# SBUF placement of a decoder trunk's tiles: weights and activations at multiples of 2048 bytes, the recurrence's tiles at the top, the MLP's tiles below

## The chip, the cores and the metric

The kernel runs on one core of a Trainium2 chip. A core has a matrix engine (PE, with its weight loads listed apart as PEld), a vector engine (DVE), a scalar engine (ACT), a general engine (POOL) and a queue engine (SP) that issues nearly all transfers here. SBUF is the on-chip memory: 128 partitions, each with its own bytes numbered from 0; a tile of 128 x 512 f32 takes 2048 consecutive bytes in every partition. PSUM holds what PE writes. The metric is the device time of one execution in microseconds.

A matmul has two operands in SBUF. The stationary one (128 x 128, 512 bytes per partition) is loaded into PE ahead of the matmul, by an instruction that the profile calls LDWEIGHTS, while the matmul before it is still streaming its moving operand (here 128 x 512, 2048 bytes per partition).

## The reference

One layer of a decoder trunk over 2048 tokens of width 1024, followed by a norm; all in f32:

```python
h = rmsnorm(x, norm_mix_w) * (1 + sc1) + sh1          # sc, sh, g: silu(c) @ ada_w + ada_b
proj = h @ w_in                                       # 1024 -> 3624
o_a = hgrn2_mixer(hq, hf, hi, hg, ...)                # gated linear recurrence, 4 heads, chunks
o_b = dsa_mixer(sq, sk, sv, iq, ik, iw)               # indexer, top-256 keys per query, softmax
o_c = conv_module(cu, ...)                            # GLU, causal depthwise conv, LayerNorm, swish
x = x + g1 * (concat[o_a, o_b, o_c] @ w_out)
h = rmsnorm(x, norm_mlp_w) * (1 + sc2) + sh2
x = x + g2 * (square(relu(h @ mlp_w1)) @ mlp_w2)
return rmsnorm(x, final_norm_w)
```

## The kernel before

Tokens go in four blocks of 512. For each block the normed x is transposed into eight tiles of 128 x 512 and split into a high part `ah` and a low part `al` (both fp32r, 8 buffers each, pool `act`). Each product of f32 matrices is then three fp32r products: high x high, high x low, low x high. Weights are fetched into `wraw`, split by ACT and POOL into `whi` and `wlo`, written to DRAM once (`wk_d`) and read back by later blocks as `wk` into the same buffers (pool `wts`). The program has two stages.

- The in-projection of all four blocks (`in_block`, matmuls of `mm_T`, L424, and `n_part`, L1280). Between its units run the recurrence (`hgrn_gen`), the convolution and, for the first six query blocks, the indexer, top-k and attention with tiles of the pool `tk1`. The recurrence's tiles are in the pool `hgrn`.
- The out-projection and the MLP of the four blocks (`mlp_block`). `mm_T` (L424) makes the hidden layer: stationary a 128 x 128 piece of a weight tile, moving a tile of `ah` or `al`. `wide_part` (L1304) makes the second product and the out-projection: stationary a 128 x 128 piece of a hidden tile (`hh`, `hl`) or of a mixer output (`mh`), moving a weight tile of 128 x 512. In the last block seven of eight groups run as Strassen products (`product`, L1464; stationary a piece of `hc`, moving a weight tile). The remaining query blocks run between these, with tiles of the pool `tk2`.

All addresses in SBUF come from the pools. A pool is opened on the left (upwards from the lowest free byte) or on the right (downwards from the top) and is closed as a stack; tiles lie in it in the order in which the program first asks for them, each on a multiple of 32 bytes. The left side begins with `cst` (constants), then `act`, `wts` and `xio` (tiles of x, `xt` and `tf`). The other pools take turns: `hgrn` (left) and `tk1` (right) live in the first stage; `mlp` (right) takes the place of `tk1` when the last of its query blocks is done, `mlpacc` (the accumulator `acc`) and `tk2` (both left) take the place of `hgrn`. A pool that takes over memory waits for the last users of what lay there, tile by tile.

Where the tiles that feed the large matmuls start, in bytes of a partition (buffers of one kind follow each other at multiples of 2048):

| tile | pool | role at L424 | role at L1304 and L1464 | start | start modulo 2048 | start modulo 128 |
|---|---|---|---|---|---|---|
| ah, al | act | moving | - | 20448 | 2016 | 96 |
| wraw, whi, wlo, wk | wts | stationary | moving | 53216 | 2016 | 96 |
| hh, hl, mh, hc | mlp | - | stationary | 185216 | 896 | 0 |

At L424 the moving tile and every stationary piece (512 bytes apart) are a whole multiple of 128 bytes away from each other. At L1304 and L1464 the stationary piece starts 32 bytes past a whole multiple of 128 from the moving tile. The accumulator `acc` starts at 98528; `qi`, `ki`, `qs`, `kc`, `vc` and `pT` of the attention start at other remainders in `tk1` than in `tk2`.

The order of the instructions is set by a scheduler that plays a timeline of the program when it is built; the row lists of the engines below come from there.

`exact_rows` (its three words `cd`, `rj`, `c4`) is a branch for queries whose search does not close; it is taken only when a register says so.

Of the kernel before, what the change touches and what calls it, by code (L numbers as in the profile page):

```python
# [8 lines left out]
F32 = mybir.dt.float32  # L9
# [5 lines left out]
U32 = mybir.dt.uint32  # L15
# [5 lines left out]
P = 128  # L21
# [57 lines left out]
def trunk(ctx, tc, x, c, ada_w, ada_b, norm_mix_w, norm_mlp_w, w_in, hg_lb_logits,  # L79
# [12 lines left out]
    cst = ctx.enter_context(tc.tile_pool(name="cst", bufs=1))  # L92
# [48 lines left out]
    def dram(shape, dt, name):  # L141
# [23 lines left out]
                    fill=NEG_BIG, base=0, channel_multiplier=1)  # L165
# [262 lines left out]
    def in_norm(b):  # L428
        xts = []
        for t in range(4):  # L430
            xt = xp.tile([P, D], F32, tag="xt", bufs=4, name=nm("xt"))
            dma(xt, x2d[b * TB + t * P:b * TB + (t + 1) * P, :])
            dump = xp.tile([P, D], BF16, tag="tf", bufs=2, name=nm("xdump"))
            rs = rstd_of(xt, D, dump, "x")
            V.tensor_scalar(xt, xt, rs, None, op0=OP.mult)
            xts.append(xt)
        return xts


    S1 = ExitStack()  # L440
    S1b = ExitStack()
    hp = S1.enter_context(tc.tile_pool(name="hgrn", bufs=1))
    tp = S1b.enter_context(tc.tile_pool(name="tk1", bufs=1, side="right"))

    iw_s = cst.tile([P, 16, 8], F32, name="iw_s")
    S_st = [hp.tile([P, P], F32, name=f"S_st{h}") for h in range(HH)]
# [14 lines left out]
    zq = cst.tile([P, 14], F32, name="zq")  # L461
    gq_ = cst.tile([P, 14], F32, name="gq_")
    i8 = cst.tile([P, 8], F32, name="i8")

    def search_consts():


        w = hp.tile([P, 5, 14], F32, tag="cu", bufs=2, name="sconst")
        ii = hp.tile([P, 14], mybir.dt.int32, tag="fb", bufs=FBB, name="sint")
        na, p_, q_, a_, b_ = [w[:, i] for i in range(5)]  # L470
        G.iota(ii, pattern=[[P, 14]], base=2 * P + 1, channel_multiplier=1)
        V.tensor_copy(na, ii)
        V.reciprocal(p_, na)
        V.tensor_scalar(gq_, p_, 0.683, None, op0=OP.mult)
        V.tensor_scalar(p_, p_, float(TOPK), None, op0=OP.mult)
        V.tensor_scalar(q_, p_, -1.0, 1.0, op0=OP.mult, op1=OP.add)
        V.memset(na, LAM)
        G.tensor_tensor(a_, p_, na, OP.pow)
        G.tensor_tensor(b_, q_, na, OP.pow)
        V.tensor_tensor(zq, b_, a_, OP.subtract)  # L480
        V.tensor_scalar(zq, zq, 5.0633, None, op0=OP.mult)
        V.reciprocal(p_, p_)
        V.reciprocal(q_, q_)
        V.tensor_tensor(a_, a_, p_, OP.mult)
        V.tensor_tensor(b_, b_, q_, OP.mult)
        V.tensor_tensor(a_, a_, b_, OP.add)
        V.tensor_tensor(gq_, gq_, a_, OP.mult)
        i8i = hp.tile([P, 8], mybir.dt.int32, tag="fb", bufs=FBB, name="i8i")
        G.iota(i8i, pattern=[[1, 8]], base=0, channel_multiplier=0)
        V.tensor_scalar(i8, i8i, 0.5, None, op0=OP.add)  # L490
# [265 lines left out]
    def ada_gen():  # L756
        for sec, dst in ((2, None), (4, a2), (3, sh2), (5, None)):
            for c0 in range(0, D, AW):
                acc = hp.tile([P, AW], F32, tag="ada", bufs=1, name=nm("adacc"))
                yield from ada_part(hp, "adw", AB, acc, sec, c0, AW)  # L760
                if dst is None:
                    pt = ps_xp(13)
                    T.matmul(pt[:1, :AW], ones, acc, start=True, stop=True)
                    row = hp.tile([1, AW], F32, tag="adw", bufs=AB, name=nm("adrow"))
                    dma(row, ada_b[0:1, sec * D + c0:sec * D + c0 + AW])
                    V.tensor_tensor(row, pt[0:1, :AW], row, OP.add)
                    dma(g_d[sec][:, c0:c0 + AW], row)
                else:
                    ada_col(acc, sec, c0, AW, dst)
            if sec == 4:  # L770
                ada_scale(a2, "nmlp")
# [9 lines left out]
    def nkeys(j):  # L781
        return (j + 1) * P
# [43 lines left out]
    def exact_rows(k, j, s, bt, dump, cum, cnt, d):  # L826


        n = nkeys(j)
        bv = bt[:, :n]  # L830
        cd, rj, c4 = [k.t([P, 1], U32, tag, 1) for tag in ("cd", "rj", "c4")]
        V.tensor_copy(bv.bitcast(U16), s.bitcast(U16).rearrange("p (n two) -> p n two", two=2)[:, :, 1])
        V.memset(cd, 0xBFFFFFFF)
        V.memset(c4, 0x40000000)
        V.tensor_scalar(dump, s, 0.0, 0.0, op0=OP.is_ge, op1=OP.add, accum_out=cnt)
        V.tensor_scalar(rj, cnt, float(TOPK), None, op0=OP.is_ge)
        V.copy_predicated(cd, rj, c4)
        for bit in range(30, 15, -1):
            V.tensor_scalar(dump, bv, cd.bitcast(BF16)[:, 1:2], 0.0, op0=OP.is_ge, op1=OP.add, accum_out=cnt)
            V.tensor_scalar(rj, cnt, float(TOPK), float(1 << bit), op0=OP.is_lt, op1=OP.mult)  # L840
            V.tensor_scalar(cd, cd, 1 << (bit - 1), rj, op0=OP.bitwise_xor, op1=OP.bitwise_xor)
        cdh = cd.bitcast(U16)
        sm = k.t([P, 6], F32, "sm", 1)
        hv, neg, sgn, off, need, zc = [sm[:, i:i + 1] for i in range(6)]
        V.tensor_copy(hv, cdh[:, 1:2])
        V.tensor_scalar(neg, hv, 32768.0, None, op0=OP.is_ge)
        V.tensor_scalar(sgn, neg, -2.0, 1.0, op0=OP.mult, op1=OP.add)
        V.tensor_scalar(off, neg, 65535.0, None, op0=OP.mult)
        V.tensor_scalar(dump, bv, cd.bitcast(BF16)[:, 1:2], 0.0, op0=OP.is_gt, op1=OP.add, accum_out=cnt)
        V.tensor_scalar(need, cnt, -1.0, float(TOPK), op0=OP.mult, op1=OP.add)  # L850
        z = cum.bitcast(U16)[:, :n]
        V.tensor_scalar(z, s.bitcast(U16).rearrange("p (n two) -> p n two", two=2)[:, :, 0], sgn, off,
                        op0=OP.mult, op1=OP.add)
        V.scalar_tensor_tensor(z, bv.bitcast(U16), hv, z, op0=OP.is_equal, op1=OP.mult)
        V.memset(zc, 32768.0)
        for bit in range(15, -1, -1):
            V.tensor_scalar(bv, z, zc, 0.0, op0=OP.is_ge, op1=OP.add, accum_out=cnt)
            V.tensor_scalar(cnt, cnt, need, float(1 << bit), op0=OP.is_lt, op1=OP.mult)
            V.tensor_scalar(zc, zc, float(1 << (bit - 1)) if bit else 0.0, cnt,
                            op0=OP.add, op1=OP.subtract)  # L860
        V.tensor_scalar(zc, zc, sgn, off, op0=OP.mult, op1=OP.add)
        V.tensor_copy(cdh[:, 0:1], zc)
        v = cd.bitcast(F32)
        V.tensor_scalar(dump, s, v, 0.0, op0=OP.is_gt, op1=OP.add, accum_out=cnt)
        V.tensor_scalar(cnt, cnt, -1.0, float(TOPK), op0=OP.mult, op1=OP.add)
        V.tensor_scalar(bv, s, v, None, op0=OP.is_equal)
        V.tensor_tensor_scan(cum[:, :n], bv, bv, 0.0, op0=OP.add, op1=OP.max)
        V.scalar_tensor_tensor(bv, cum[:, :n], cnt, bv, op0=OP.is_le, op1=OP.mult)
        V.scalar_tensor_tensor(dump, s, v, bv, op0=OP.is_gt, op1=OP.add)
        V.memset(d, TOPK - AIM - (PASSES - 1) * STEP)  # L870
# [316 lines left out]
    S2 = ExitStack()  # L1187
    k1 = TK(tp, J1 * P, SB)

    def add_topk(k, js):  # L1190
        for j in js:
            queues["idx"].append(index_gen(k, j))
            queues["tk"].append(topk_gen(k, j))
# [402 lines left out]
    for b in range(NB):  # L1596
        def nxt(b=b):
            if b + 1 < NB:
                xq.append(in_norm(b + 1))
        for ev in in_block(b, xq[b], nxt):  # L1600
            if ev == "idx":
                if b == 0:
                    add_topk(k1, (2, 3))
                if b == 1:
                    add_topk(k1, range(4, J1))
                    queues["ada"].append(ada_gen())
            elif ev == "qkv":
                pass
            elif ev == "prep":
                drain("ada")  # L1610
                drain_bg()
                S1b.close()
                mp = S2.enter_context(tc.tile_pool(name="mlp", bufs=1, side="right", reuse_waits="tile"))
                prep_out(0)
            else:
                step()
            if ev == "qkv":
                qdone.append(b)
                if b == 0:
                    queues["at"] += [attn_gen(k1, 0), attn_gen(k1, 1)]  # L1620
# [4 lines left out]
    SP.close()  # L1625
    px["p"] = S2.enter_context(tc.tile_pool(name="psy", bufs=1, space=PSUM, reuse_waits="tile"))
    px["ax"] = AXB
    mq = S2.enter_context(tc.tile_pool(name="mlpacc", bufs=1, reuse_waits="tile"))
    S3 = ExitStack()
    tp2 = S3.enter_context(tc.tile_pool(name="tk2", bufs=1, reuse_waits="tile"))  # L1630
    k2 = TK(tp2, 2048, SB)
    add_topk(k2, ORDER)
    rates.update({"idx": R2[0], "tk": R2[1], "at": R2[2]})
# [33 lines left out]
```

## Time and profile before

| | |
|---|---|
| median of 3 runs | 2909.93 us (2903.92 to 2911.09) |
| the profiled execution, its own time | 2909.95 us |
| its span, first to last instruction | 2908.2 us |
| mean granted clock of PE | 0.984 |
| DMA packets, bytes | 428074, 688.61 MB, 237 GB/s over the span |
| matmul records of 128 x 512 at L424, L1304, L1464 | 5280, 3072, 588 |

The profiled execution lies 0.02 us from the median, so a sum made against its span carries over: 1.7 us lie outside the span. Durations of matmuls in the profile overlap, since their ends are modelled; how far apart they start is read from the timeline and from stretches in which one kind runs alone.

### The profile page before, as it was taken

The numbers are of one execution on the slowest core, as the hardware profiler recorded it, in microseconds if no ns is written. First come the engines' busy times: TensorE is split into PE (matmuls) and PEld (weight loads), VectorE is DVE, ScalarE is ACT, GpSimd is POOL, SyncE is SP. The second block draws the span as 40 slices with busy tenths as digits, with TensorE's granted clock in tenths as the row PEclk, the third lists the DMA queues.
The fourth block names the chain that finished last, engine by engine and source line by source line (L and its number), as shares of the span: only waits on it lengthen the run. The fifth ranks groups of instructions, "written<-read, shape, count | busy, mean of one in ns | idle before, by whom it ended". The sixth has DMA issues, their size and how long they took to land.

```text
span 2908.2 us, 42801 instructions
## 1 busy us (share of the span) xinstructions
PE 2781.8 (96%) x14116; PEld 2306.0 (79%) x14116; DVE 1676.6 (58%) x3514; ACT 1239.7 (43%) x2630; POOL 1086.4 (37%) x1051
## 2 busy tenths in 40 slices
PE   5999998999999989999999999999999998999997
PEld 4888887888788777888777888887788887777776
DVE  6695697777465437656757637477662221254455
ACT  4436444533311244555556444354643332343323
POOL 7444111212100445666665222234422223345444
PEclk9999999999999989999999999999999999999999
DMA  9987676667655668898888776677867666686676
GB/s 292 291 268 243 215 234 190 218 209 245 202 183 180 221 218 255 272 291 284 292 266 295 231 221 216 202 243 258 289 211 237 200 226 197 217 284 209 224 235 206
DMA packets 428074, 688.61 MB, mean 237 GB/s; under 512 B 43383, under 2 KB 171452, under 8 KB 427836
## 3 DMA queue, kind: packets, MB, share of 16 engines
q1 hardware_dynamic: 427680, 685.67, 72.9%
q8 instruction: 113, 1.85, 0.3%
q14 instruction: 125, 1.02, 0.1%
q10 hardware_dynamic: 156, 0.07, 0.0%
HBM read 532.74 MB, written 152.84 MB: 236 GB/s over the span
## 4 chain that ended last, share of the span: by engine, by line
PE 41%; DMA 5%; DVE 4%; POOL 1%; issue 1%; ACT 0%; SPq 0%; POOLq 0%; DVEq 0%; ACTq 0%
PE mm L1304 10%; PE mm L424 9%; PE ax L424 7%; PE ax L1304 6%; PE mm L1464 4%; PE at L965 1%; PE po L999 1%; DMA wk<-wk_d 1%; PE at L987 1%; PE ix L808 1%; DMA tr<-in_mlp_w_dram 1%; PE at L1304 1%; DVE s L815 1%; DVE cum L917 1%; POOL wk L376 1%
## 5 line engine op out<-in xcount | busy, mean ns | idle before, releaser
L424 PE MATMUL mm<-ah,wk 128*128 128x512 f32 x1920 | 513.2, 399 | 4.1 <-DVE slo L537 1.7
L424 PEld LDWEIGHTS mm<-ah,wk 128*128 128x128 f32 x1920 | 355.7, 190 | 78.5 <-DVE slo L537 2.0
L318 POOL TENSOR_TENSOR wlo<-wraw,whi 128x512 fp32r<-128x512 f32 x210 | 285.8, 1380 | 245.2 <-ACT whi L317 133.6
L997 POOL TENSOR_TENSOR pT<-L,pT 128x512 fp32r<-128x512 f32 (+3 forms) x160 | 193.3, 1210 | 374.9 <-ACT pT L996 194.3
L815 DVE SCALAR_TENSOR_TENSOR s<-r,iw_s,s 128x512 f32<-128x512 f32 (+3 forms) x266 | 239.2, 899 | 104.2 <-ACT r L810 95.6
L424 PE MATMUL mm<-al,wk 128*128 128x512 f32 x960 | 262.4, 395 | 0.0
L967 DVE CUSTOM_DVE_ANT_0 L<-at,bias 128x512 f32<-128x512 f32 (+3 forms) x152 | 93.6, 619 | 206.0 <-PE at L965 156.7
L424 PEld LDWEIGHTS mm<-al,wk 128*128 128x128 f32 x960 | 178.3, 189 | 36.0
L1304 PE MATMUL mm<-wk,hh 128*128 128x512 f32 x640 | 197.8, 398 | 1.5 <-ACT tf L286 1.1
L810 ACT ACTIVATE r<-ix 128x512 f32<-128x512 f32 (+3 forms) x256 | 133.2, 554 | 151.6 <-PE ix L808 113.0
L317 ACT CAST whi<-wraw 128x512 fp32r<-128x512 f32 x210 | 122.1, 620 | 162.6 <-DMA wraw<-in_mlp_w_dram 47.9
L273 POOL TENSOR_TENSOR hl<-hr,hh 128x512 fp32r<-128x512 f32 x96 | 129.6, 1351 | 161.3 <-ACT hh L265 159.5
L424 PE MATMUL ax<-ah,wk 128*128 128x512 f32 x720 | 187.1, 393 | 1.4 <-DMA wk<-wk_d 1.4
L588 DVE SCALAR_TENSOR_TENSOR cx<-hc,cvc,cx 128x512 f32<-128x512 f32 x232 | 173.7, 749 | 2.0
L917 DVE TENSOR_SCALAR_CACHE_REDUCE cum<-s,ssm 128x384 bf16<-128x384 f32 (+13 forms) x112 | 165.3, 1476 | 7.3 <-POOL s L819 5.2
L995 ACT COPY L<-at 128x512 f32<-128x512 f32 (+3 forms) x160 | 82.8, 522 | 180.6 <-PE at L987 179.0
L424 PEld LDWEIGHTS ax<-ah,wk 128*128 128x128 f32 x720 | 134.2, 188 | 31.2 <-ACT hc L1438 1.8
L1464 PE MATMUL mm<-wk,hc 128*128 128x512 f32 x588 | 148.4, 397 | 4.9 <-DVE acc L1472 4.9
L981 ACT ACTIVATE L<-L,nmx 128x512 f32<-128x512 f32 (+3 forms) x160 | 103.8, 650 | 97.9 <-DVE nmx L976 97.7
L1304 PEld LDWEIGHTS mm<-wk,hh 128*128 128x128 f32 x640 | 117.9, 188 | 27.4 <-ACT tf L286 1.6
L1464 PEld LDWEIGHTS mm<-wk,hc 128*128 128x128 f32 x588 | 109.4, 188 | 35.3 <-DVE acc L1472 8.7
L1304 PE MATMUL ax<-wk,hh 128*128 128x512 f32 x384 | 123.8, 400 | 1.7 <-DMA wk<-wk_d 1.4
(364 smaller groups left out, 6096.4 us busy)
## 6 DMA issues: line engine op xcount, KB each, us to landing
wk<-wk_d SPq DMA_DIRECT2D x776, 256.0 KB
wk<-wk_d SPq DMA_DIRECT2D x196, 512.0 KB
wk_d<-whi SPq DMA_DIRECT2D x210, 256.0 KB
wk_d<-wlo SPq DMA_DIRECT2D x210, 256.0 KB
wraw<-in_mlp_w_dram SPq DMA_DIRECT2D x68, 512.0 KB
kc<-sk_d SPq DMA_DIRECT2D x112, 256.0 KB
vc<-v_d SPq DMA_DIRECT2D x112, 256.0 KB
adw<-in_ada_w_dram SPq DMA_DIRECT2D x128, 128.0 KB
```

Source lines behind the costliest of these rows:

```text
L273: e.tensor_tensor(lo[:, i:j], src[:, i:j], hi[:, i:j].bitcast(F32), OP.subtract)
L317: A.copy(hi, src)
L318: G.tensor_tensor(lo, src, hi.bitcast(F32), OP.subtract)
L424: T.matmul(ps, ww[k], aa[k], start=(n == 0 and k0 == 0), stop=(n == len(order) - 1 and k1 == NK))
L588: V.scalar_tensor_tensor(acc if w < TAPS - 1 else total, hc[:, w:w + TB], cvc[:, m, w:w + 1], acc, op0=OP.mult, op1=OP.add)
L810: A.activation(r[:, :w], ps[:, :w], AF.Relu, scale=32.0 ** -0.5)
L815: V.scalar_tensor_tensor(s[:, c0:c0 + w], r[:, :w], iw, s[:, c0:c0 + w], op0=OP.mult, op1=OP.add)
L917: V.tensor_scalar(dump, s, t, -AIM - i * STEP, op0=OP.is_ge, op1=OP.add, accum_out=d)
L981: A.activation(lt[:, :w], lt[:, :w], AF.Exp, bias=nmx, accum_out=sm[:, cb:cb + 1])
L997: G.tensor_tensor(pT[:, :nt, 1], lv, pT[:, :nt, 0].bitcast(F32), OP.subtract)
L1304: T.matmul(ps, aa[f][:, tok * P:(tok + 1) * P], ww[i], start=(first and n == 0), stop=(last and n == 5))
L1464: T.matmul(bank[t], aa[:, k, t * P:(t + 1) * P], ww[k], start=(i in (0, 2, 4) and n == 0), stop=(n == 5), skip_group_check=True)
```

## The change

The sides of the pools are exchanged: `hgrn` opens on the right and `tk1` on the left; later `mlp` on the left, in the place of `tk1`, and `mlpacc` and `tk2` on the right, in the place of `hgrn`. A tile of 32 bytes (`fill`) is added to the constants, so that everything behind them moves up by 32 bytes. The three words of `exact_rows` become columns of one tile.

```diff
-    hp = S1.enter_context(tc.tile_pool(name="hgrn", bufs=1))
-    tp = S1b.enter_context(tc.tile_pool(name="tk1", bufs=1, side="right"))
+    hp = S1.enter_context(tc.tile_pool(name="hgrn", bufs=1, side="right"))
+    tp = S1b.enter_context(tc.tile_pool(name="tk1", bufs=1))
...
     i8 = cst.tile([P, 8], F32, name="i8")
+    cst.tile([P, 8], F32, name="fill")
...
-        cd, rj, c4 = [k.t([P, 1], U32, tag, 1) for tag in ("cd", "rj", "c4")]
+        words = k.t([P, 3], U32, "words", 1)
+        cd, rj, c4 = [words[:, i:i + 1] for i in range(3)]
...
-                mp = S2.enter_context(tc.tile_pool(name="mlp", bufs=1, side="right", reuse_waits="tile"))
+                mp = S2.enter_context(tc.tile_pool(name="mlp", bufs=1, reuse_waits="tile"))
...
-    mq = S2.enter_context(tc.tile_pool(name="mlpacc", bufs=1, reuse_waits="tile"))
+    mq = S2.enter_context(tc.tile_pool(name="mlpacc", bufs=1, side="right", reuse_waits="tile"))
     S3 = ExitStack()
-    tp2 = S3.enter_context(tc.tile_pool(name="tk2", bufs=1, reuse_waits="tile"))
+    tp2 = S3.enter_context(tc.tile_pool(name="tk2", bufs=1, side="right", reuse_waits="tile"))
```

The starts after the change:

| tile | start before | start after | after, modulo 2048 | after, modulo 128 |
|---|---|---|---|---|
| ah, al | 20448 | 20480 | 0 | 0 |
| wraw, whi, wlo, wk | 53216 | 53248 | 0 | 0 |
| tf, xt, tr, xo | 77792 | 77824 | 0 | 0 |
| hh, hl, mh, hc | 185216 | 98560 | 256 | 0 |
| acc | 98528 | 212960 | 2016 | 96 |

So at L424 the moving tile and the stationary piece keep their distance, a whole multiple of 128. At L1304 and L1464 the distance becomes a whole multiple of 128 too (before: 32 past one).

Apart from the three words, which become one tile, no engine's sequence changes: the same instructions stand in the same order. What changes besides the addresses is which semaphores a few instructions wait for where one pool takes over the memory of another. The largest such place is on SP at the begin of the MLP of the first block, where `tk2` takes the memory of `hgrn`. `qi`, `ki`, `qs`, `kc` and `vc` are tiles of the first query block in `tk2`, `mx_d` is the last output of the recurrence; names in brackets are semaphores (DMAHW: transfers, PE_49: the matrix engine). Before:

```order
L107 DMA mx_d_3_122<-r_11503 128x512 [waits DMAHW1_49,DVE_49]
L107 DMA qi_11653<-iq_d_76 32x8x128 [waits DMAHW2_49,PE_49]
L107 DMA qi_11653<-iq_d_76 32x8x128 [waits DMAHW3_49]
L107 DMA qi_11653<-iq_d_76 32x8x128 [waits DMAHW4_49]
L107 DMA ki_11658<-ki_d_87 96x512 [waits DMAHW5_49]
L107 DMA qs_12996<-sq_d_80 64x4x128 [waits DMAHW6_49]
```

And now:

```order
L107 DMA mx_d_3_122<-r_11496 128x512 [waits DMAHW1_49,DVE_49]
L107 DMA qi_11646<-iq_d_76 32x8x128 [waits DMAHW2_49]
L107 DMA qi_11646<-iq_d_76 32x8x128 [waits DMAHW3_49]
L107 DMA qi_11646<-iq_d_76 32x8x128 [waits DMAHW4_49]
L107 DMA ki_11651<-ki_d_87 96x512 [waits DMAHW5_49,PE_49]
L107 DMA qs_12987<-sq_d_80 64x4x128 [waits DMAHW6_49]
```

The wait for PE has moved from the first `qi` to `ki`; in the same way it moves a little further on from the first `vc` to the first `kc`. On DVE the first write of `s` (L814 now, L813 before) gains a wait for two transfers and loses none; on ACT, POOL and DVE some twenty other instructions at such places wait for fewer or for other transfers.

## The prediction

> **What bounds the kernel now.** I read the busy shares first, then the slices.
>
> ```profile
> PE 2781.8 (96%) x14116; PEld 2306.0 (79%) x14116; DVE 1676.6 (58%) x3514; ACT 1239.7 (43%) x2630; POOL 1086.4 (37%) x1051
> PE   5999998999999989999999999999999998999997
> ```
>
> PE is busy for 96% of the span, in nearly every slice for nine tenths or more; no other engine passes 58%. All PE idle time together is 2908.2 - 2781.8 = 126 us. So what a change of addresses does to PE's own pace counts almost in full, and what it does to the other engines counts only where PE then waits. The second view is the sum of one line's matmuls over the whole span.
>
> ```profile
> 0.00:2910.00 2910.00, 781.47 (x3072) 0.98 0.73 237
> 0.00:2910.00 2910.00, 148.35 (x588) 0.98 0.73 237
> 0.00:2910.00 2910.00, 1301.69 (x5280) 0.98 0.73 237
> ```
>
> These are L1304, L1464 and L424 in this order: 3072 + 588 + 5280 = 8940 matmuls of 128 x 512, the bulk of PE's time. Their durations in the view by line (min/median/max in ns) differ:
>
> ```profile
> L424 PE MATMUL mm<-ah,wk x1920: 387/389/796, 261.3 to 2568.5; 128*128 128x512 f32 x192
> L424 PE MATMUL mm<-al,wk x960: 387/389/628, 261.6 to 2566.7; 128*128 128x512 f32 x192
> ...
> L1304 PE MATMUL mm<-wk,hh x640: 388/394/505, 1597.7 to 2543.3; 128*128 128x512 f32 x160
> ...
> L1304 PE MATMUL mm<-wk,mh x288: 388/394/482, 1432.7 to 2494.4; 128*128 128x512 f32 x144
> ...
> L1464 PE MATMUL mm<-wk,hc x588: 388/394/505, 2574.2 to 2869.3; 128*128 128x512 f32 x196
> ```
>
> The same size and type takes 389 ns at L424 and 394 ns at L1304 and L1464, whatever the tile. Ends are modelled, so I check it by starts. In the timeline of PE two stretches meet where each kind runs alone and no idle time stands between:
>
> ```profile
> 2475.32 3.19 PE L1304 MATMUL mm<-wk,mh 128*128 128x512 f32 x13
> ...
> 2494.68 2.00 PE L424 MATMUL mm<-ah,wk 128*128 128x512 f32 x8
> ...
> 2516.46 0.60 PE L281 MATMUL mm<-ident,x 128*128 128x128 f32 x4
> ...
> 2475.32:2494.67 19.35, 19.35 (x84) 1.00 0.66 220
> 2494.68:2516.45 21.77, 21.77 (x96) 1.00 0.86 293
> ...
> 2839.83 0.40 PE L424 MATMUL ax<-ah,wk 128*128 128x512 f32 x1
> 2840.07 2.96 PE L1464 MATMUL mm<-wk,hc 128*128 128x512 f32 x12
> 2842.87 0.63 PE L424 MATMUL ax<-ah,wk 128*128 128x512 f32 x2
> ```
>
> L1304: 83 starts (the count of 84 holds the one still running when the stretch begins) from 2475.32 to 2494.68, **233.3 ns** each. L424: 96 from 2494.68 to 2516.46, **226.9 ns**. L1464: 12 in 2842.87 - 2840.07 = 2.80 us, 233.3 ns. The granted clock is 1.00 in both stretches, and the transfers are heavier (293 against 220 GB/s) in the faster one, so neither the clock nor the transfers make the 6.4 ns. What differs is the kind of work and the addresses: at L424 moving tile and stationary piece are a whole multiple of 128 bytes apart, at L1304 and L1464 they are not (the table of starts).
>
> **The change part by part.** *The exchange of sides and the 32 bytes of fill.* No instruction is added or moved, so each term is a pace. At L1304 and L1464 the distance between the moving tile and the stationary piece becomes a whole multiple of 128, as at L424. My reading is that the weight load of the next matmul, which runs while a tile streams, costs the stream some cycles at the old distance and few at a multiple of 128. Then these 3072 + 588 = 3660 matmuls take L424's pace: 3660 x 5 ns (medians) = **18.3 us**; by the dense stretches 3660 x 6.4 = 23.4 us. I take the medians, since most of these matmuls stand among others and not in dense runs. L424 keeps its distance and so its pace: 0.
>
> How much reaches the end? PE's waits and the densest stage tell:
>
> ```profile
> PE at L1304 <- DMA wk<-wk_d: 7.4, 3, 5.6
> PE mm L1304 <- DVE acc L1557: 4.9, 3, 4.0
> PE mm L1464 <- DVE acc L1472: 4.9, 8, 1.4
> ...
> 1200.00:1550.00 350.00, 177.43 (x698) 129.44 (x697) 0.99 0.88 279
> 1550.00:1900.00 350.00, 159.85 (x622) 113.84 (x620) 1.00 0.73 234
> 1900.00:2250.00 350.00, 170.68 (x672) 122.86 (x672) 1.00 0.75 247
> ```
>
> The largest waits at L1304 are 7.4 us for weights and 4.9 for the accumulator, of 781 us. If PE gets 2% quicker there, the weight transfers are late next. From 1550 us on they are busy for 0.73 to 0.75 of the time and have room. From 1200 to 1550 us the share is 0.88; there I count nothing as gained: 698 x 5 ns = 3.5 us. That leaves 18.3 - 3.5 = **14.8 us**. Were the cover gone everywhere, half might be lost.
>
> *The same addresses for the other engines.* ACT and POOL already run one operation at different remainders:
>
> ```profile
> L317 ACT CAST whi<-wraw 128x512 fp32r<-128x512 f32 x210 | 122.1, 620 | 162.6 <-DMA wraw<-in_mlp_w_dram 47.9 <-PE mm L424 32.5 <-DMA wraw<-in_w_in_dram 19.2
> L265 ACT CAST hh<-hr 128x512 fp32r<-128x512 f32 x96 | 59.6, 624 | 2.2
> L318 POOL TENSOR_TENSOR wlo<-wraw,whi 128x512 fp32r<-128x512 f32 x210 | 285.8, 1380 | 245.2 <-ACT whi L317 133.6 <-PE mm L424 38.5 <-PE mm L1280 21.6
> L273 POOL TENSOR_TENSOR hl<-hr,hh 128x512 fp32r<-128x512 f32 x96 | 129.6, 1351 | 161.3 <-ACT hh L265 159.5 <-DMA wk<-wk_d 1.7
> ```
>
> At 2016 modulo 2048 (first and third row) and at 896 (the others) they take 620 and 624 ns, 1380 and 1351 ns: 2% at most. At remainder 0 the trace has no row; by these I put it between -2% and +2% of engines that are 43% and 37% busy, under PE: 0 us.
>
> *The waits where pools take over.* On SP `ki` now waits for PE where `qi` did.
>
> ```profile
> L748 PE MATMUL ax<-ident,hu x64: 270/272/477, 174.4 to 1078.4; 128*128 128x128 f32 x64
> L622 DVE SCALAR_TENSOR_TENSOR cu<-cacc,cols,cu x8: 742/752/753, 301.4 to 1033.0; 128x512 f32<-128x512 f32 x8
> ...
> 1080.12 1.41 SPq L107 DMA_DIRECT2D qi<-iq_d  x3
> 1081.57 0.45 SPq L107 DMA_DIRECT2D ki<-ki_d  x1
> ```
>
> The recurrence's last matmul starts at 1078.4 us and takes 0.3; `ki` is issued at 1081.57, so the wait is over before it is reached. Queued behind it on SP are `qs` and the stores of `wk_d`, which the same holds for. The first write of `s` now waits for transfers of tiles such as the convolution's `cu`, last made at 1033.0 us, also long landed. I take 0; bounds: -1.4 us (the longest wait of SP there, one issue of `qi`, gone) to +1.4 (the same, gained).
>
> *The three words.* The lines of `exact_rows` have no row in the trace: the branch isn't taken. 0.
>
> *Attention in new places.* Distances of `qi`, `qs`, `vc` to the tiles before them change in both directions. It is some hundred weight loads behind a tile of 512; at 6.4 ns a hundred are 0.6 us, either way: 0.
>
> **Sum:** 2909.95 - 14.8 = 2895.1, said as **2895 us**; the execution is 0.02 us from the median, so nothing is added. Own range of this case: -23.4 (dense pace, all of it kept) to -9 (half of 18.3 lost): 2886.5 to 2901.
>
> **The rivals.** *No effect.* The 6.4 ns may belong to the kind of work: L424 adds 24 matmuls into one PSUM tile in a row, L1304 and L1464 six at a time, with activations as the stationary operand and weights as the moving one. One set of rows speaks for it:
>
> ```profile
> L1280 PE MATMUL mm<-whi,ah x96: 277/283/668, 81.4 to 221.9; 128*128 128x256 f32 x96
> ...
> L1280 PE MATMUL mm<-whi,hh x80: 278/282/286, 2870.1 to 2890.0; 128*128 128x256 f32 x80
> ```
>
> At L1280, with 256 columns, the stationary piece of `hh` (off by 32) is no slower than that of `ah` (a multiple of 128): 282 against 283 ns. Against it: each kind loads one stationary piece per matmul, so PE's steps are the same; and the single L424 matmul ahead of the L1464 run, whose stream meets the load of a piece of `hc`, takes 2840.07 - 2839.83 = 0.24 us, some ten ns above L424's own pace, though its own work is L424's. The timeline rounds to 0.01 us, so this is a hint and no proof. Time: 2909.95, between 2906 and 2914 with what runs vary. The Trainium skill's page "SBUF — State Buffer", section "Who interferes with whom", speaks for this rival: it gives PE two independent read ports, one for the moving operand and one for weight loads, and says that PE never waits on anyone. By it the sum would be 0; the trace shows two paces for one size, but no row says whether the addresses make them.
>
> *Slower: the weight tile's own address counts, not the distance.* At L1304 and L1464 every stationary piece starts on a multiple of 128 bytes and is slow; at L424 it starts 96 past one and is fast. The rows fit this as well. After the change L424's pieces start on multiples of 128 too: 5280 x 5 ns = 26.4 us are added, nothing is gained at L1304: 2936. It decides as soon as a round start alone is enough. Against it: at L1280 pieces of `hh` start on multiples of 128 and cost nothing (282 ns). I hold the distance for likelier, since two reads that meet need two addresses.
>
> *Faster still: the start of the moving tile counts.* 512 columns take 226.9 ns; 256 take 120.0 (below), so 256 columns are 106.9 and each matmul has 226.9 - 213.8 = 13.1 ns that its columns don't need.
>
> ```profile
> 2882.92 0.64 PE L1280 MATMUL ax<-wlo,hh 128*128 128x256 f32 x4
> 2883.40 1.12 PE L1280 MATMUL ax<-whi,hh 128*128 128x256 f32 x8
> 2884.36 0.64 PE L1280 MATMUL ax<-wlo,hh 128*128 128x256 f32 x4
> ```
>
> (12 matmuls in 2884.36 - 2882.92 = 1.44 us.) All moving tiles of weights and activations start 32 bytes before a multiple of 2048 now and on one afterwards. If that took a quarter of the 13.1 ns, 8940 x 3.3 = 29 us would come on top: 2866; all of it would be 117 us. For it: no row has a tile at 0. Against: nothing shows that these nanoseconds are reading.
>
> **How the numbers follow.** Forecast (2886.5 to 2901) 0.54; no effect, within 2906 to 2914, 0.21; slower by the weight's own address 0.15; faster still 0.10. A measurement of this kernel can tell about 0.3%, 8.7 us, from no change. The forecast and the last case lie beyond it: faster 0.64; no effect: same 0.21; slower 0.15. The range takes the forecast, the case of no effect with its variation, and the case of faster still down to its quarter: 2866 to 2916. It leaves out the slower case and more than half of the faster one, together 2 in 10.
>
> **What would show it.** Right: medians at L1304 and L1464 fall from 394 to about 389, dense stretches from 233.3 to about 227 ns, L424 stays at 389 and 226.9. No effect: all medians stay. Slower: L424 rises to 394. Faster still: L424 falls below 387. If the medians fall and the time does not, the waits of PE for `wk` or `acc` at L1304 have grown by what was gained. The forecast is wrong at its root if L1304 keeps 394 ns.

## The result and the profile after

| | before | after |
|---|---|---|
| median | 2910.51 us (2903.92 to 2912.61, 4 runs) | 2892.19 us (2887.88 to 2895.25, 4 runs) |
| ratio, 95% interval | | 0.9946 [0.9927, 0.9964] |
| span of the profiled execution | 2908.2 us | 2886.1 us |

By the medians the kernel is 18.3 us faster, by the ratio 15.7 us; the forecast was 2895 us, 15 us faster. Timed again later beside other kernels, it was 11.2 us faster by the medians, 2896.68 against 2907.87 us, and 14.0 us by the ratio, 0.9952 [0.9935, 0.997]. Lines behind the diff have moved: L1304 is L1306 now, L1464 is L1466; L424 keeps its number.

The busy shares and the slices of PE, after:

```profile
PE 2757.0 (96%) x14116; PEld 2297.4 (80%) x14116; DVE 1671.6 (58%) x3514; ACT 1240.7 (43%) x2630; POOL 1086.6 (38%) x1051
PE   5999998999999989999999999999999999999997
```

PE's busy time fell from 2781.8 to 2757.0 us, 24.8 us, with the same 14116 instructions. The other engines stand where they stood to within 5 us. PE's idle time is 2886.1 - 2757.0 = 129 us, against 126 before: 3 us more. The durations by line (min/median/max in ns; first and last start in us):

```profile
L424 PE MATMUL mm<-ah,wk x1920: 387/389/632, 259.3 to 2548.4; 128*128 128x512 f32 x192
...
L1306 PE MATMUL mm<-wk,hh x640: 387/389/499, 1586.1 to 2523.3; 128*128 128x512 f32 x160
...
L1306 PE MATMUL mm<-wk,mh x288: 387/389/485, 1421.9 to 2475.3; 128*128 128x512 f32 x144
...
L1466 PE MATMUL mm<-wk,hc x588: 387/389/504, 2554.1 to 2846.7; 128*128 128x512 f32 x196
```

394 ns has become 389 at L1306 and L1466; L424 keeps 389. The busy time of L1306, L1466 and L424 over the whole span, in this order:

```profile
0.00:2920.00 2920.00, 771.47 (x3072) 0.99 0.73 236
0.00:2920.00 2920.00, 144.99 (x588) 0.99 0.73 236
0.00:2920.00 2920.00, 1295.07 (x5280) 0.99 0.73 236
```

Against the rows of before these are -10.0, -3.4 and -6.6 us. The same dense stretch as in the prediction, in the timeline of PE (start, length, line, operation):

```profile
2456.70 3.15 PE L1306 MATMUL mm<-wk,mh 128*128 128x512 f32 x13
...
2475.56 1.98 PE L424 MATMUL mm<-ah,wk 128*128 128x512 f32 x8
...
2497.32 0.60 PE L281 MATMUL mm<-ident,x 128*128 128x128 f32 x4
```

And by windows, the first with L1306 alone, the second with L424 alone (length, busy time of PE and count, the same of PEld, granted clock, DMA share, GB/s):

```profile
2456.70:2475.56 18.86, 18.86 (x84) 15.39 (x82) 1.00 0.67 222
...
2475.56:2497.34 21.78, 21.78 (x96) 17.84 (x95) 1.00 0.84 294
```

83 starts at L1306 in 18.86 us are **227.2 ns** each (233.3 before); 96 at L424 in 2497.32 - 2475.56 = 21.76 us are 226.7 (226.9 before). The two kinds of work now run at one pace, at the same granted clock of 1.00 and under the same load of transfers as before.

The waits of PE that the prediction named show that no new wait took the gain:

```profile
PE at L1306 <- DMA wk<-wk_d: 7.3, 4, 4.5
PE mm L1466 <- DVE acc L1474: 6.1, 7, 1.9
...
PE mm L1306 <- DVE acc L1559: 5.1, 3, 4.0
```

They were 7.4, 4.9 and 4.9 us.

**Where in the span the time came from.** Four starts divide the program: the last matmul of the recurrence (`ax<-ident,hu`), the first and the last `mm<-wk,hh`, and the last `mm<-wk,hc`. For the changed kernel the first of them is here (the others stand above):

```profile
L749 PE MATMUL ax<-ident,hu x64: 270/272/474, 174.3 to 1068.9; 128*128 128x128 f32 x64
```

The last `hu` starts at 1068.9 us, 9.5 us earlier than before. Of the matmuls with a new pace only the 192 for the first part of the out-projection have run by then; at 4.5 ns each they explain 0.9 us. Most of the 9.5 us is there even before the first of them starts (first row before, second after):

```profile
L1304 PE MATMUL at<-whi,mh x64: 389/394/499, 962.0 to 1014.8; 128*128 128x512 f32 x64
L1306 PE MATMUL at<-whi,mh x64: 387/389/499, 954.6 to 1006.6; 128*128 128x512 f32 x64
```

In a second profiled execution of the same kernel (c1_after below) this lead is missing:

```profile
L749 PE MATMUL ax<-ident,hu x64: 270/273/476, 174.3 to 1077.7; 128*128 128x128 f32 x64
L1306 PE MATMUL mm<-wk,hh x640: 387/389/526, 1597.0 to 2537.2; 128*128 128x512 f32 x160
L1466 PE MATMUL mm<-wk,hc x588: 387/389/713, 2568.0 to 2860.3; 128*128 128x512 f32 x196
```

So most of the early 9.5 us are not the change's. The mean granted clock was 0.987 in the first of these two executions and 0.984 in the second, as in the profile of before:

```profile
core 0: 2886.1 us, clock 0.987
```

```profile
core 0: 2898.5 us, clock 0.984
```

In the 31 runs of the kernel before that stand beside the first four experiments, time and granted clock go together (correlation -0.82, 2.1 us less for each 0.001 of clock), so 0.003 are some 6 us. One profile of each kernel would have credited them to the change. By these rows, as means over executions with the old and the new pace at L1306:

| stage | before, b0, e8 | after, c1, e2, c2 | gain |
|---|---|---|---|
| start to the last `hu` | 1079.4 us | 1075.1 us | 4.3 |
| to the first `mm<-wk,hh` | 518.9 | 518.1 | 0.8 |
| to the last `mm<-wk,hh` | 947.6 | 940.1 | 7.6 |
| to the last `mm<-wk,hc` | 326.0 | 323.0 | 3.0 |

Within one column the values spread by 6 to 10 us in the first stage, so its 4.3 us are no finding; by 1 to 2 us in the second, 3 to 6 in the third and 1 in the fourth. The second stage is the one under heavy transfers (share 0.88 between 1200 and 1550 us, before and after); it holds 966 matmuls of L1304 and gave nearly nothing. The split by stages is weak, though. The kernel e3 below is back at the slow pace and shows 1079.6, 519.1, 942.6 and 324.3 us; e1 and e9, also slow, show 515.1 and 515.4 us in the second stage, less than any execution at the new pace. So stages move by 3 us and more for reasons that these rows don't show, and what follows rests on the paces and on whole times.

### The profile page after: what moved, and what is told of

It reads as the page before. It is cut to its first block, busy times and chain, and to the rows that moved or that the text cites. A ratio compares the mean times of both kernels' runs of the same rounds, so it can differ in the third digit from the quotient of the medians.

```text
span 2886.1 us, 42799 instructions
## 1 busy us (share of the span) xinstructions
PE 2757.0 (96%) x14116; PEld 2297.4 (80%) x14116; DVE 1671.6 (58%) x3514; ACT 1240.7 (43%) x2630; POOL 1086.6 (38%) x1051
## 4 chain that ended last, share of the span: by engine, by line
PE 45%; DMA 4%; DVE 4%; POOL 2%; issue 1%; ACT 1%; SPq 0%; POOLq 0%; DVEq 0%; ACTq 0%
PE mm L1306 11%; PE mm L424 10%; PE ax L424 7%; PE ax L1306 6%; PE mm L1466 3%; PE at L967 2%; PE po L1001 2%; PE at L989 1%; PE ix L809 1%; DMA wk<-wk_d 1%; DMA tr<-in_mlp_w_dram 1%; PE at L1306 1%; DVE s L816 1%; POOL wk L376 1%; DVE cum L919 1%
## 5 line engine op out<-in xcount | busy, mean ns | idle before, releaser
L424 PE MATMUL mm<-ah,wk 128*128 128x512 f32 x1920 | 509.4, 396 | 4.9 <-ACT tf L286 1.9
L424 PEld LDWEIGHTS mm<-ah,wk 128*128 128x128 f32 x1920 | 353.6, 188 | 77.7 <-ACT tf L286 2.1
L424 PE MATMUL mm<-al,wk 128*128 128x512 f32 x960 | 262.3, 395 | 0.0
L424 PEld LDWEIGHTS mm<-al,wk 128*128 128x128 f32 x960 | 177.9, 188 | 35.4
L1306 PE MATMUL mm<-wk,hh 128*128 128x512 f32 x640 | 196.0, 395 | 2.1 <-ACT tf L286 1.1
L424 PE MATMUL ax<-ah,wk 128*128 128x512 f32 x720 | 185.4, 391 | 1.8 <-ACT hc L1440 1.4
L424 PEld LDWEIGHTS ax<-ah,wk 128*128 128x128 f32 x720 | 134.1, 188 | 30.2 <-ACT hc L1440 1.8
L1466 PE MATMUL mm<-wk,hc 128*128 128x512 f32 x588 | 145.0, 392 | 6.9 <-DVE acc L1474 6.1
L1306 PEld LDWEIGHTS mm<-wk,hh 128*128 128x128 f32 x640 | 118.0, 188 | 26.8 <-ACT tf L286 1.7
L1466 PEld LDWEIGHTS mm<-wk,hc 128*128 128x128 f32 x588 | 109.4, 188 | 34.1 <-DVE acc L1474 10.0
L1306 PE MATMUL ax<-wk,hh 128*128 128x512 f32 x384 | 122.6, 397 | 1.5 <-DMA wk<-wk_d 1.1
```

The lines of the kernel that those rows point to most:

```text
L424: T.matmul(ps, ww[k], aa[k], start=(n == 0 and k0 == 0), stop=(n == len(order) - 1 and k1 == NK))
L1306: T.matmul(ps, aa[f][:, tok * P:(tok + 1) * P], ww[i], start=(first and n == 0), stop=(last and n == 5))
L1466: T.matmul(bank[t], aa[:, k, t * P:(t + 1) * P], ww[k], start=(i in (0, 2, 4) and n == 0), stop=(n == 5), skip_group_check=True)
```

## The experiments

Theories. **Distance**: the pace of a 128 x 512 matmul depends on how far the stationary piece lies from the moving tile, modulo 128 as the prediction says, or another period. **Round start**: a start on a multiple of 2048 makes it. **Place**: the MLP's tiles low and the rest high. Distances below are the start of the stationary piece less that of the moving tile, modulo 256; before it is 0 at L424 and 160 at L1304 and L1464, after it is 0 at all.

**e1_fill_only**: the sides of before, with the fill and the words; the distance at L1306 is 128.

```diff
     i8 = cst.tile([P, 8], F32, name="i8")
+    cst.tile([P, 8], F32, name="fill")
...
+        words = k.t([P, 3], U32, "words", 1)
+        cd, rj, c4 = [words[:, i:i + 1] for i in range(3)]
```

> The pools stay on the sides of before; only the 32 bytes of fill and the three words in one tile are taken from the change. Low tiles then start at 0 modulo 2048, the MLP's tiles stay at 185216, and the distance from moving tile to stationary piece at L1304 and L1464 is 0 modulo 128 (128 modulo 256). Distance theory (the pace follows the distance modulo 128): median 389 ns at both lines, 2888 to 2897 us, the whole gain. Round-start theory (the low tiles' start at a multiple of 2048 is what counts): the same 389 and 2892. Place theory (the MLP's tiles must lie low, the others high): 394 ns as before, 2910. A distance theory with a period of 256 would also give about 394.

Measured 2901.09 us, ratio 0.9974 [0.9953, 0.9995]. Medians by line:

```profile
L1306 PE MATMUL mm<-wk,hh x640: 387/394/505, 1594.2 to 2542.2; 128*128 128x512 f32 x160
```

The slow pace stays at a distance of 128: the period is 256, not 128, and low tiles at 2048 alone don't bring the fast pace. That the time fell by some 8 us all the same (0.0026 of 2910) is taken up under e9.

**e2_no_fill**: the changed kernel without the fill; low tiles at 2016 modulo 2048, all distances 0.

```diff
-    cst.tile([P, 8], F32, name="fill")
```

> The change without its 32 bytes of fill: low tiles at 2016 modulo 2048 as before, the MLP's tiles just above them at 98528, so that the distance at L1304 and L1464 stays 0 modulo 128 though no tile starts on a round number. Distance theory: median 389 ns, 2888 to 2897 us, the whole gain. Round-start theory: 394 ns, about 2910. Place theory: 389, about 2892.

Measured 2897.5 us, ratio 0.9964 [0.995, 0.9979]; busy 771.71 us at L1305 (L1306 of the changed kernel), 145.03 at L1465, with medians of 389 ns. Round start falls.

**e3_mlp_32**: the changed kernel with 32 bytes ahead of the MLP's tiles; place and round starts as after, the distance at L1306 and L1466 is 32.

```diff
                 mp = S2.enter_context(tc.tile_pool(name="mlp", bufs=1, reuse_waits="tile"))
+                mp.tile([P, 8], F32, name="shift")
```

> The change with 32 bytes more ahead of the MLP's tiles (98592): low tiles still at 0 modulo 2048, the distance at L1306 and L1466 becomes 32 modulo 128 as it was before. Distance theory: median back at 394 ns at both lines, 3660 x 5 to 6.4 ns = 18 to 23 us lost, 2907 to 2915 us; L424 stays at 389. Round-start theory and place theory: 389 ns, about 2892.

Measured 2906.06 us, ratio 0.9997 [0.9978, 1.0015]: no gain over before is left, and the time lies just below the 2907 to 2915 us expected.

```profile
L1306 PE MATMUL mm<-wk,hh x640: 389/395/503, 1598.7 to 2541.3; 128*128 128x512 f32 x160
...
L1466 PE MATMUL mm<-wk,hc x588: 389/395/504, 2572.1 to 2865.6; 128*128 128x512 f32 x196
```

32 bytes take the pace back at just these two lines (L424 keeps 389 ns). Place falls too.

**e4_act_32**: the fill moved between `act` and `wts`; the distance at L424 becomes 32, at L1306 it stays 0.

```diff
     wp = ctx.enter_context(tc.tile_pool(name="wts", bufs=1))
+    wp.tile([P, 8], F32, name="fill")
...
-    cst.tile([P, 8], F32, name="fill")
```

> The change with its 32 bytes of fill put between the activations and the weights: ah and al at 2016 modulo 2048 as before, weights and all that is above them as in the change. The distance at L424 becomes 32 modulo 128, at L1306 and L1466 it stays 0. Distance theory: L424 rises from 389 to 394 ns, L1306 and L1466 stay at 389; 5280 x 5 to 6.4 ns = 26 to 34 us lost, 2916 to 2926 us. Round-start theory: L424 slower too, if a moving tile's start at 2016 is what costs, but before it ran at 389 ns with that start, so 389 and 2892. Place theory: 389, about 2892.

Measured 2912.33 us, ratio 1.0006 [0.9987, 1.0024]. The projections (L425 here) by line:

```profile
L425 PE MATMUL mm<-ah,wk x1920: 387/395/775, 260.5 to 2575.9; 128*128 128x512 f32 x192
```

Their busy time over the whole span, by a window:

```profile
0.00:2920.00 2920.00, 1319.79 (x5280) 0.99 0.72 236
```

The cost can be put on a line that never had it: 395 ns, and 24.7 us more than the 1295.07 of after. Medians at L1306 and L1466 stay at 389. The time is 4 us below the range expected: not all of the added PE time reaches the end.

**e5, e6, e7**: constants of 32 and 64 bytes are moved from `cst` to the front of `wts` (which shifts L424's distance) and to `xio` (which shifts the MLP's). For e5:

```diff
     wp = ctx.enter_context(tc.tile_pool(name="wts", bufs=1))
+    wp.tile([P, 8], F32, name="fill")
+    i8 = wp.tile([P, 8], F32, name="i8")
...
-    lbc = cst.tile([P, 4], F32, name="lbc")
-    oml = cst.tile([P, 4], F32, name="oml")
+    lbc = xp.tile([P, 4], F32, name="lbc")
+    oml = xp.tile([P, 4], F32, name="oml")
...
-    zq = cst.tile([P, 14], F32, name="zq")
-    gq_ = cst.tile([P, 14], F32, name="gq_")
-    i8 = cst.tile([P, 8], F32, name="i8")
-    cst.tile([P, 8], F32, name="fill")
+    zq = xp.tile([P, 14], F32, name="zq")
+    gq_ = xp.tile([P, 14], F32, name="gq_")
```

> The low tiles are shifted against each other with constants of 32 and 64 bytes that change pools: distance from the moving tile to the stationary piece 64 modulo 256 at the matmuls of the projections (L424 of the changed kernel), 192 at the MLP's (L1306, L1466). Theory 'only 0 modulo 256 is free': all of these take 394 to 396 ns (median), both lines cost what e3 and e4 showed, 2892 + 18 + 20 = 2930 us. Theory 'some distances are free, others not' (0 free; 32, 128, 160 not): one or both of 64 and 192 stay at 389 ns; the attention scores in the changed kernel, at a distance of 192, show 225 ns between starts, so 192 at the MLP's lines would stay at 389 or below, and L424 alone is open: 2892 to 2912 us.

> As e5_64_192 with the distances 96 modulo 256 at L424 and 224 (that is, -32) at L1306 and L1466. Theory 'only 0 modulo 256 is free': 394 to 396 ns at all of them, 2930 us. Theory 'some distances are free': odd multiples of 32 were slow so far (32, 160), so 96 and 224 are slow too by it, 2930 us; a line at 389 ns here would say that the sign of the distance counts, or that the free places are single ones.

> As e5_64_192 with the distances 128 modulo 256 at L424 and 64 at L1306 and L1466. If the distance alone decides, whatever the kind of matmul, L424 is as slow as the MLP's lines were at 128 in e1 (393 to 395 ns, L424's busy time about 1320 us instead of 1295), and the MLP's lines show what L424 shows at 64 in e5. 'Only 0 modulo 256 is free': 394 to 396 ns at both, 2930 us. 'Some are free': 64 as L424 at 64; with 64 free 2912 us.

One run of each: 2918.02, 2922.24 and 2922.67 us, beside 2914.58 of before. All lie 7 to 12 us below the 2930 expected; with single runs, and runs of before spread over 13 to 23 us in the other comparisons, only the paces are read here. By line, e5:

```profile
L426 PE MATMUL mm<-ah,wk x1920: 388/395/775, 266.2 to 2581.3; 128*128 128x512 f32 x192
...
L1306 PE MATMUL mm<-wk,hh x640: 387/393/506, 1608.5 to 2555.5; 128*128 128x512 f32 x160
```

The busy time of e5's L1306, by a window:

```profile
0.00:2920.00 2920.00, 774.79 (x3072) 0.98 0.72 236
```

e6:

```profile
L427 PE MATMUL mm<-ah,wk x1920: 387/397/796, 261.5 to 2583.2; 128*128 128x512 f32 x192
...
L1306 PE MATMUL mm<-wk,hh x640: 388/395/505, 1603.3 to 2557.3; 128*128 128x512 f32 x160
```

e7:

```profile
L427 PE MATMUL mm<-ah,wk x1920: 387/393/775, 262.9 to 2582.2; 128*128 128x512 f32 x192
...
L1306 PE MATMUL mm<-wk,hh x640: 387/394/503, 1605.5 to 2556.5; 128*128 128x512 f32 x160
```

A median hides sizes, since durations hang on modelled ends. The start-to-start mean of neighbouring matmuls of one line (gaps under 260 ns, so without waits and throttled ones) is sharper: executions at one distance agree within 0.2 ns at the MLP's second product. In ns, by distance:

| distance modulo 256 | L424 | second product (L1304, L1306) | L1464, L1466 | from |
|---|---|---|---|---|
| 0 | 228.3 to 228.8 | 228.9 to 229.0 | 227.3 to 228.8 | after, c1, e2, c2, e4; L424 elsewhere too |
| 32 | 233.1 | 232.9 | 232.8 | e4; e3 |
| 64 | 233.2 | 233.3 | 232.5 | e5; e7 |
| 96 | 234.0 | | | e6 |
| 128 | 232.6 | 232.6 | 232.6 to 232.7 | e7; e1, e9 |
| 160 | | 233.4 to 233.6 | 233.5 | before, b0, e8 |
| 192 | | 229.8 | 231.7 | e5 |
| 224 | | 233.1 | 233.2 | e6 |

Only 0 is free. Where a distance was measured at both, it costs nearly the same at L424 as at the MLP's lines (within 1 ns), so the kind of work has no visible part in it. "Some distances are free" falls, with 192 as a cheap one: its median is 393 ns, but at L1306 its mean is 0.9 ns over the fast pace. No distance at these lines is faster than 0, so none of them gives a better version. The 225 ns of the attention's scores, from which the expectation of e5 argued for 192, stay unexplained.

**c1_after and c2_no_fill**: the changed kernel and e2_no_fill once more, on one chip.

> The changed kernel once more, beside the same kernel without the 32 bytes of fill (c2_no_fill) on one chip, since in the first runs the two stood 5 us apart with intervals that overlap. Theory 'the fill is worth nothing, the distance of 0 modulo 256 is all': both give the same time within 0.2%, about 2892 to 2897 us, and the same busy time at L424 within 3 us. Rival 'a start on a multiple of 2048 is worth some 5 us at L424': this kernel 2892, the other 2897 us, L424 busy 1295 against 1300 us.

> The changed kernel without the fill: all low tiles 32 bytes lower, the distances at the 128 x 512 matmuls 0 modulo 256 as with it. By 'the fill is worth nothing' the time of c1_after within 0.2% (5.8 us), medians of 389 ns at all three lines. By the rival 5 us more than c1_after, with the busy time at L424 about 5 us higher and the MLP's lines the same.

Measured 2896.68 us, ratio 0.9952 [0.9935, 0.997], and 2899.24 us, ratio 0.9959 [0.9944, 0.9974]; L424 is busy for 1297.44 and 1296.77 us. The fill is worth nothing that can be told.

**b0_before, e8_words_only, e9_fill_again**: before against itself, before with the words alone, and e1 again.

> The kernel before, unchanged, timed against itself, since e1_fill_only and e3_mlp_32 came out 9 and 4 us below it although their MLP matmuls kept the slow pace. Theory 'the comparison itself is even': ratio 1, 2908 to 2911 us. Rival 'the kernel that is compared comes out lower by its place in the rounds': 2903 to 2906 us, a ratio of about 0.998, and every gain above would be smaller by that.

> Before with the three words in one tile and nothing else: the tiles of the second top-k and of attention (kc, qs, ki, qi, vc, pT) move by 32 bytes among themselves, the low tiles stay at 2016 modulo 2048, the MLP's lines at the slow distance of 160. Theory 'the words do nothing': 2908 to 2911 us, medians of 394 ns at the MLP's lines. Rival 'part of what e1_fill_only won is from the attention's tiles': 2903 to 2907 us.

> e1_fill_only once more, beside the two others. Medians of 394 ns at the MLP's lines as before. If its gain of 9 us was variation: a ratio within 0.998 and 1.002 here; if the fill or the words win something beside the MLP's pace: 2901 to 2904 us again, and e8_words_only tells which of the two.

Measured 2908.91, 2910.2 and 2903.98 us; ratios 0.9999 [0.9986, 1.0011], 0.9999 [0.9986, 1.0011] and 0.9978 [0.9963, 0.9993]. The comparison is even, the words do nothing, and the gain of the fill on the old sides is real: by the ratios 6 us, 8 in e1. Start-to-start means would give 5.2 us of it: in e1 and e9 the MLP's lines go from 233.4 to 232.6 ns (160 to 128: 3660 x 0.85 = 3.1 us) and L424 from 228.75 to 228.35 (5280 x 0.4 = 2.1 us). By the stages it lies elsewhere, 3.7 us of it in the second, where 966 x 0.85 = 0.8 us are expected. So its cause stays open, and it matters: a kernel whose MLP lines keep a slow pace already has about half of the 13 us that the changed kernels gain on average (below).

## Why the prediction was right, point by point

**PE bounds, and a change of pace counts.** Right: PE is busy for 96% before and after, and its idle time has grown by 3 us only.

**The reading of the distance.** Right in kind, too short in period: the fast pace needs a multiple of 256, not of 128 (e1, e7). Tiles are 2048 bytes apart, pieces 512, so the change had brought 256 along with 128. The prediction didn't ask for that: here it had luck, since e1, which meets its condition of 128, keeps the slow pace. It needs no more than 256: in the changed kernel the second product's distance is 98560 - 53248 = 45312 bytes, 256 modulo 512, and L424's is 32768, 0 modulo 512; both are fast.

That it is the *next* matmul's stationary piece is seen in e3, where L424's own distance is 0 and that from `ah` to a piece of `hc` is 32: in the last block an L424 matmul takes 227.3 ns when another of L424 follows and 235.5 when one of L1466 does (590 and 52 of them by starts, gaps under 260 ns). But a slow pair also disturbs its neighbours, as a group of seven L424 matmuls between two runs of L1464 shows. Before:

```profile
2842.87 1.78 PE L424 MATMUL ax<-ah,wk 128*128 128x512 f32 x7
2844.49 2.96 PE L1464 MATMUL mm<-wk,hc 128*128 128x512 f32 x12
```

After:

```profile
2842.64 1.75 PE L424 MATMUL ax<-ah,wk 128*128 128x512 f32 x7
2844.23 2.88 PE L1466 MATMUL mm<-wk,hc 128*128 128x512 f32 x12
```

1.62 us have become 1.59, 231 ns each against 227, though L424's own distance is 0 in both. Taken by starts over the whole traces, the last of such a group, followed by L1464, takes 234.6 ns before and 226.6 after (51 and 51 of them). But in before the first two L424 matmuls behind a run of the MLP's lines are slow too, 234.1 and 233.7 ns (227.1 and 227.4 after), and it takes some ten until 226.7 is reached. And an L1464 matmul followed by L424, where moving tile and next piece are both weight tiles and a multiple of 512 apart, takes 229.7 ns before and 232.8 in e3, against 226.8 after. So the slow step begins with the moving tile and the piece that is loaded behind it, but one pair's distance doesn't give its pace alone: the steps before it count. How the delay is carried on no record shows. That the two reads meet is the simplest account of this, and argued: no record shows the meeting itself.

**The size, 18.3 us by medians.** By start-to-start means it is 3072 x (233.4 - 228.9) = 13.8 and 588 x (233.5 - 227.4) = 3.6, 17.4 us. The medians were the right choice; the dense stretches (23.4 us) were too much, as was reasoned.

**3.5 us taken off for the stage under heavy transfers.** The number agrees, the reason isn't shown. Between the last `hu` and the first `wk,hh` 966 matmuls became 4.5 ns quicker, 4.3 us, and 0.8 us arrived, so 3.5 were lost; the forecast had counted the 698 in the window of 350 us. But e1 and e9 gained 3.7 us in this very stage with a pace only 0.85 ns quicker, so transfers alone can't be read from it. That a part of PE's time doesn't reach the end is seen in e4 as well: 5280 x 4.85 ns = 25.6 us were added, and its ratio stands 0.0054 to 0.0060 above those of the changed kernel, 16 to 17 us. Where the rest went isn't shown.

**L424 at 0.** Not quite: it became 0.4 to 0.5 ns quicker, 2.4 us of 5280. Its distance was 0 already. All kernels with the fill or with exchanged sides have this, where L424's distance is 0; before, b0 and e8 have not. Most of it is the after-effect told above: the L424 matmuls that follow a run of the MLP's lines with no other kind between (some 870 of 4650 gaps) take 228.8 ns in before, b0 and e8 and 226.8 to 226.9 in the changed kernels; the other L424 matmuls take 228.7 to 228.8 and 228.6 to 228.7.

**The sum of 14.8 us.** The two timings give 18.3 and 11.2 us by medians, 15.7 and 14.0 by ratios; with e2 and c2, which have the same distances, the mean ratio is (0.9946 + 0.9952 + 0.9964 + 0.9959) / 4 = 0.9955, 13 us. The forecast lies within. That it is this close is partly luck: PE's pace gave 17.4 + 2.4 = 19.8 us, 1.5 us more than the sum began with, and about 7 us of it, not 3.5, did not arrive.

**Other engines, waits, words and attention at 0.** Right. DVE, ACT and POOL moved by -5.0, +1.0 and +0.2 us of busy time. The last `hu` matmul starts at 1068.9 us, and `ki`, which now waits for PE, is issued after it without delay behind `qi`:

```profile
1070.58 1.46 SPq L107 DMA_DIRECT2D qi<-iq_d  x3
1072.13 0.39 SPq L107 DMA_DIRECT2D ki<-ki_d  x1
```

The words alone give 0.9999 (e8).

**The rivals.** *No effect*: refuted, by e3 and e4 above all, which switch the pace by 32 bytes at one kind of line and leave the other. The Trainium skill's page "SBUF — State Buffer", section "Who interferes with whom", says that the two read ports of PE are independent and that PE waits on nobody. By it the addresses would make no difference; the traces don't agree, with 229 against 233 ns for one shape by addresses alone. Whether it is the ports that interfere no run shows. *The weight tile's own address*: refuted, L424 stayed at 389 with its pieces on multiples of 128, and e2 has the fast pace at 2016 modulo 2048. *Faster still*: refuted, 226.7 against 226.9 ns in the dense stretch of L424, and no difference between c1 and c2. The 13.1 ns beyond the columns remain.

## What to carry to other kernels

Where matmuls like these (128 x 512 f32) follow each other densely, lay the moving tiles and the stationary pieces of the next matmul a multiple of 256 bytes apart in the partition; a constant of 32 bytes between two pools cost about half a per cent here (e3, e4). When one shape has two paces, compare addresses modulo a few powers of two before looking for a cause in the work, and use starts instead of durations. Before a gain is placed in a profile, look at stages that the change hardly touches, and at other kernels with the old pace: what moves there is the size of the variation.

## What the runs showed of the hardware

- A 128 x 512 matmul starts 227.3 to 229.0 ns behind the last one at a distance of 0 modulo 256 (means of a line), and 232.5 to 234.0 at 32, 64, 96, 128, 160 and 224; at 192 it is between (229.8 and 231.7).
- The delay lasts beyond the pair that makes it: behind a run at a distance of 160 the first two L424 matmuls at a distance of 0 took 234.1 and 233.7 ns, against 227.1 and 227.4 behind a run at 0.
- Time goes with the granted clock, about 2 us for each 0.001 (31 runs of one kernel); 0.003 between two executions are some 6 us, half the gain of this edit.
- In the stage with a DMA share of 0.88 a quicker PE gained 0.8 of 4.3 us on the mean; kernels with a slow pace move by as much there, so the loss can't be put on the transfers.
